# The scaled queries of the attention heads get the idle tiles of the raw weights' parts, and the first head's scores stand one unit later

## The chip, the cores and the metric

The kernel runs on one core of a Trainium2 chip. A core has a matrix engine (TensorE, PE in the profile, with PEld for its weight loads), three engines for elementwise work (VectorE is DVE, ScalarE is ACT, GpSimd is POOL) and a queue that issues the transfers from memory (SyncE, SP). Each engine carries out its own instructions in the order in which they were written for it, and waits on semaphores for the others. The metric is the time of one execution on the device in microseconds (us).

## The reference, cut to what matters

One layer of a streaming encoder works on 256 frames of width 2048 in float32: a half-step feed-forward part, a mixer, a cross attention over 256 memory tokens, and a second half-step feed-forward part. The change lies in the mixer:

```python
h = rms_norm(x, mix_norm[l])
proj = h @ w_in[l]
u, q, k, v, g, a_lr = jnp.split(proj, list(IN_SPLITS), axis=-1)
y_pool = pool_mixer(u, pool_w[l], pool_scale[l])
y_gla = gla_mixer(q, k, v, g, a_lr, gla_w_a2[l], gla_b_a[l], gla_head_norm[l])
x = x + jnp.concatenate([y_pool, y_gla], axis=-1) @ w_out[l]
```

The pool mixer takes, in four groups of channels, the trailing mean over 2, 4, 8 or 16 frames minus the frame itself, and multiplies each group with its own small matrix. The linear attention has four heads and works in four chunks of 64 frames: every frame of a chunk sees its whole chunk and all earlier ones, and each earlier chunk is weakened by the products of the decays in between.

## The kernel before, in words

**Units.** The whole kernel is one stream of units. A unit is one megabyte of weights: SyncE loads it into one of three `raw` tiles (`load`, line 1578), ScalarE rounds it to a high part `wh` (line 1602) and VectorE takes the difference to a low part `wl` (line 453), and TensorE multiplies with both parts, which gives a product near float32. The parts of two units ahead are made before the products of a unit are written (`AHEAD`, line 41), and there are three buffers of `wh` and `wl`, so the high part of a unit waits until TensorE is done with the unit three before it. Between the units stand operations that were handed in with `st.op(f, after)`: `f` is written `after` units later.

**Which instruction stands where on an engine.** The source is written in that order, but a planner then orders each engine's instructions by its own estimate of when they can start (line 1631). So an operation can be moved between the products of a unit. Parts of the weights keep their own order (`in_turn`).

**Tiles.** A pool tile has a tag and a number of buffers. A new tile with a tag takes the buffer whose last reader is done, and its first writer waits for that reader. In the mixer three buffers with the tag `m4` go round (`m4`, line 977). They hold the sums of the pool groups (`ev_pool`, line 986: the token tile `u` and two tiles `s0`, `s1` for the doubled sums), the intermediate results of the decay (`decay`, line 1067), the scaled queries of the heads (`scores`, line 1142) and the heads' outputs. In the profile all of these appear as `m`.

**Seven products.** Some units are multiplied with seven products in place of eight, and for these VectorE makes sums of the weights; the parts of the raw weights are then kept in tiles with the tags `xh` and `xl` (`split_seven`, line 471). In the mixer one tile of each stands ready (line 950), 128 x 1536 elements, and two units of the first block, which computes q and k, use them. After that block they have no use until the mixer ends.

**The order of the mixer.** q and k (block of eight units), the decay's low-rank gate, two blocks of four units for the pool groups (`block_a`, TensorE line 347, tile `pa`; each block ends with `ev_pool` of two groups), two blocks of four units for v (`block_b`, line 605, TensorE line 362, tile `pb`) with the pool's own weights as one unit in between (`pool_unit`, line 1018, TensorE line 1027, tile `pp`), and two blocks for the output gate. The scores of a head (`scores(h)`) copy and scale the queries into a tile with three copies on ScalarE (line 1150) and six multiplications on VectorE (line 1152), make four small float32 products on TensorE (line 1160, tile `pq`) and copy them out on VectorE (line 1166, tile `ST`).

**Where the change touches.** Before it, `scores(0)` is handed in with `after` 0. It stands between the last unit of the pool blocks and the first unit of v. The tile of its scaled queries is an `m4` tile.

## Time and profile before

| | us |
|---|---|
| median of three runs | 2090.24 |
| lowest, highest | 2089.54, 2092.51 |
| the profiled execution | 2089.89 |
| its span | 2088.1 |
| busy in the span: TensorE products | 2069.6 |
| busy in the span: VectorE | 1822.2 |
| busy in the span: ScalarE | 1152.4 |

The rows of the profile give times in us from the start of the span. A row of the timeline has a start, a length, engine, line, operation and tiles (result, arrow, operands), the number of instructions merged into it, and in brackets how long the engine stood idle before it and which instruction ended that. Names are those of the program without buffer numbers. PEclk is the share of the full clock that TensorE was granted.

### The profile page before, as it was taken

The numbers are of one execution on the slowest core, as the hardware profiler recorded it, in microseconds if no ns is written. First come the engines' busy times: TensorE is split into PE (matmuls) and PEld (weight loads), VectorE is DVE, ScalarE is ACT, GpSimd is POOL, SyncE is SP. The second block draws the span as 40 slices with busy tenths as digits, with TensorE's granted clock in tenths as the row PEclk, the third lists the DMA queues.
The fourth block names the chain that finished last, engine by engine and source line by source line (L and its number), as shares of the span: only waits on it lengthen the run. The fifth ranks groups of instructions, "written<-read, shape, count | busy, mean of one in ns | idle before, by whom it ended". The sixth has DMA issues, their size and how long they took to land.

```text
span 2088.1 us, 24282 instructions
## 1 busy us (share of the span) xinstructions
PE 2069.6 (99%) x9591; PEld 1724.6 (83%) x9591; DVE 1822.2 (87%) x1727; ACT 1152.4 (55%) x1151; POOL 100.1 (5%) x94
## 2 busy tenths in 40 slices
PE   9999999999999998999999999999999999999998
PEld 7888888888888887888888888888888888888886
DVE  7998899989998758579888887889988999889987
ACT  7655455645554664455756544566554556545554
POOL 0000000000000000000001000000100010000001
PEclk9999999999999999999999999999999999999999
DMA  7666666567666655557855555666576765676664
GB/s 263 204 200 225 237 222 220 183 222 243 222 200 223 230 176 161 162 173 231 270 193 172 172 184 178 205 204 229 188 233 205 242 208 196 225 236 227 206 227 152
DMA packets 129131, 435.94 MB, mean 209 GB/s; under 512 B 9845, under 2 KB 13529, under 8 KB 128633
## 3 DMA queue, kind: packets, MB, share of 16 engines
q1 hardware_dynamic: 128840, 433.86, 62.5%
q8 instruction: 75, 1.23, 0.2%
q10 hardware_dynamic: 176, 0.53, 0.1%
q14 instruction: 40, 0.32, 0.0%
HBM read 417.58 MB, written 16.78 MB: 208 GB/s over the span
## 4 chain that ended last, share of the span: by engine, by line
PE 98%; DVE 1%; DMA 0%; ACT 0%; issue 0%; SPq 0%; DVEq 0%; ACTq 0%
PE pt L362 59%; PE pt L507 28%; PE pa L347 4%; PE pb L362 2%; PE ph L780 1%; PE pl L1338 1%; PE pv L1375 1%; PE px L791 1%; DMA x<-in_x 0%; PE pp L1027 0%; PE pe L362 0%; DVE wl L453 0%; PE pq L1160 0%; PE pa L1054 0%; PE po L1173 0%; PE tm L1285 0%
## 5 line engine op out<-in xcount | busy, mean ns | idle before, releaser
L362 PE MATMUL pt<-wh,xs 128*128 128x512 f32 x2176 | 699.3, 391 | 0.0
L453 DVE TENSOR_TENSOR wl<-raw,wh 128x2048 fp32r<-128x2048 f32 (+1 forms) x249 | 534.0, 2152 | 117.0 <-ACT wh L1602 116.7
L1602 ACT CAST wh<-raw 128x2048 fp32r<-128x2048 f32 x249 | 475.4, 1912 | 263.3 <-PE pt L362 113.4
L362 PEld LDWEIGHTS pt<-wh,xs 128*128 128x128 f32 x2176 | 408.2, 188 | 83.7 <-ACT wh L1602 0.2
L489 ACT CAST wh<-T 128x1024 fp32r<-128x1024 f32 x250 | 262.5, 1054 | 376.1 <-DVE T L486 366.7
L362 PE MATMUL pt<-wh,ys 128*128 128x512 f32 x1440 | 455.1, 390 | 0.0
L362 PE MATMUL pt<-wl,xs 128*128 128x512 f32 x1088 | 424.8, 391 | 0.0
L362 PEld LDWEIGHTS pt<-wh,ys 128*128 128x128 f32 x1440 | 270.3, 188 | 55.6
L453 DVE TENSOR_TENSOR wl<-T,wh 128x2048 fp32r<-128x2048 f32 (+1 forms) x125 | 280.7, 2246 | 2.5 <-ACT wh L489 2.2
L362 PE MATMUL pt<-wl,ys 128*128 128x512 f32 x720 | 281.1, 391 | 0.0
L362 PEld LDWEIGHTS pt<-wl,xs 128*128 128x128 f32 x1088 | 204.6, 188 | 41.5
L280 DVE TENSOR_TENSOR xl<-raw,xh 128x1536 fp32r<-128x1536 f32 x125 | 218.9, 1751 | 13.6 <-ACT xh L279 13.5
L279 ACT CAST xh<-raw 128x1536 fp32r<-128x1536 f32 x125 | 185.0, 1480 | 59.1 <-PE pt L507 36.6
L486 DVE TENSOR_TENSOR T<-T,raw 128x512 f32<-128x512 f32 x250 | 172.5, 690 | 6.5
L362 PEld LDWEIGHTS pt<-wl,ys 128*128 128x128 f32 x720 | 135.2, 188 | 28.2 <-DVE wl L453 0.3
L486 DVE TENSOR_TENSOR T<-raw 128x1024 f32<-128x1024 f32 x125 | 152.3, 1218 | 0.5
L507 PE MATMUL pt<-wh,xs 128*128 128x512 f32 x380 | 147.9, 390 | 0.0
L457 POOL TENSOR_TENSOR wl<-raw,wh 128x768 fp32r<-128x768 f32 x42 | 78.0, 1857 | 1453.7 <-DVE wl L453 1444.6
L507 PE MATMUL pt<-xh,xs 128*128 128x512 f32 x384 | 143.4, 390 | 0.0
L507 PE MATMUL pt<-wh,xe 128*128 128x512 f32 x320 | 124.5, 389 | 0.0
L347 PE MATMUL pa<-xs,wh 128*128 128x512 f32 x256 | 90.7, 399 | 0.0
L507 PEld LDWEIGHTS pt<-xh,xs 128*128 128x128 f32 x384 | 72.1, 188 | 14.9
(256 smaller groups left out, 2360.0 us busy)
## 6 DMA issues: line engine op xcount, KB each, us to landing
raw<-in_ffn_w_down SPq DMA_DIRECT2D x88, 1024.0 KB, 5.5
raw<-in_ffn_w_up SPq DMA_DIRECT2D x80, 1024.0 KB, 5.0
raw<-in_ffn_w_gate SPq DMA_DIRECT2D x77, 1024.0 KB, 5.1
raw<-in_w_in SPq DMA_DIRECT2D x32, 1024.0 KB, 5.2
raw<-in_xattn_w_kv SPq DMA_DIRECT2D x32, 1024.0 KB, 5.1
raw<-in_w_out SPq DMA_DIRECT2D x16, 1024.0 KB, 5.6
raw<-in_xattn_w_q SPq DMA_DIRECT2D x16, 1024.0 KB, 5.5
raw<-in_xattn_w_o SPq DMA_DIRECT2D x16, 1024.0 KB, 5.5
```

What stands on the lines that cost most here:

```text
L279: in_turn("scalar", lambda: nc.scalar.copy(hi, src))
L280: in_turn("vector", lambda: nc.vector.tensor_tensor(out=lo, in0=src, in1=f32(hi), op=ALU.subtract))
L347: nc.tensor.matmul(o, w, x, start=k == 0 and i == 0, stop=last and i == 1)
L362: nc.tensor.matmul(ps, a, w, start=first and i == 0, stop=last and i == 2)
L453: in_turn("vector", lambda: nc.vector.tensor_tensor(out=lo[:, :n], in0=src[:, :n], in1=f32(hi[:, :n]), op=ALU.subtract))
L457: rest = nc.gpsimd.tensor_tensor(out=lo[:, n:], in0=src[:, n:], in1=f32(hi[:, n:]), op=ALU.subtract)
L486: in_turn("vector", lambda: nc.vector.tensor_tensor(out=o, in0=a, in1=b, op=ALU.add))
L489: in_turn("scalar", lambda: nc.scalar.copy(th[:, c], t[:, c]))
L507: nc.tensor.matmul(banks[n], x, w, start=n in fresh and j == 0, stop=n in ends and j == 2)
L780: nc.tensor.transpose(v[:, i, h * P : (h + 1) * P], g[:, h, i * P : (i + 1) * P], ident)
L791: nc.tensor.transpose(v[:, j, h * P : (h + 1) * P], x[:, h, j * P : (j + 1) * P], ident)
L1602: in_turn("scalar", lambda: nc.scalar.copy(hi, raw))
```

## The change

```diff
     def scores(h):
         q, kd, E, F = mix["q"][:, h, :], mix["k"][:, h, :], mix["E"], mix["F"]
 ...
-        QD = m4()
+        QD = scope["pool"].tile([P, 3 * NB], F32, tag=("xh", "xl")[h % 2], name=uid("QD"), bufs=1)
         at = (0, 3 * CH, 5 * CH)
 ...
-    for h, after in enumerate((0, 2, 4, 6)):
+    for h, after in enumerate((1, 2, 4, 6)):
         st.op(lambda h=h: scores(h), after)
```

The scaled queries of heads 0 and 2 go into the tile `xh`, those of heads 1 and 3 into `xl`. The `m4` buffers go round among the pool groups, the decay and the heads' outputs alone. The scores of head 0 are handed in one unit later, after the first unit of v.

No instruction is added or removed; their order changes. In the order written for the changed kernel:

- ScalarE has the copies of heads 0 and 1 right after the query tile itself, ahead of the decay's functions, those of head 2 behind the high part of v's fourth unit, and those of head 3 behind the high part of the pool's weights.
- VectorE has the twelve multiplications of heads 0 and 1 behind the factors of the decay, around the low part of the third unit of the second pool block and ahead of the low part of its fourth. The first multiplication of head 2 waits for the products of head 0, that of head 3 for those of head 1, since they take the same tile. The steps of the fourth pool group stand further apart: its first doubled sum behind the low part of v's fourth unit; the three others behind the copies (line 1166) of head 1, the multiplications of head 3 and the low part of the pool's weights; the means (lines 1001 and 1005) behind the low part of the next unit; and the group's own low part (line 286) behind the copies of head 2 and the low part of one more unit.
- TensorE goes from the last pool unit straight to the 24 products of v's first unit, then the undivided products of head 0, then v's second unit, the undivided products of head 1, v's third and fourth units, head 2, and the pool's unit. Of that unit, the products of the fourth group are split by products of the next unit of v: ten of them stand ahead of the first of the group, thirteen more ahead of the first that reads the group's low parts.
- SyncE and GpSimd have the same transfers and the same four clearings as before, in the same order.

## The prediction

> **What bounds the kernel now.** I read first the busy times and the shares of the chain that ended last:

> ```profile
> PE 2069.6 (99%) x9591; PEld 1724.6 (83%) x9591; DVE 1822.2 (87%) x1727; ACT 1152.4 (55%) x1151; POOL 100.1 (5%) x94
> PE 98%; DVE 1%; DMA 0%; ACT 0%; issue 0%; SPq 0%; DVEq 0%; ACTq 0%
> ```

> TensorE is the bound: 2069.6 us of products in a span of 2088.1, and 98% of the chain. A change gains only where TensorE stands still or runs slowly. So the next view is its waits, all of them:

> ```profile
> PE pq L1160 <- DVE m L1152: 6.6, 1, 6.6
> PE pwarm L206 <- POOL ident masks.py:199: 1.4, 1, 1.4
> PE px L717 <- DMA x<-in_x: 1.0, 1, 1.0
> PE pt L507 <- DVE xl L280: 0.2, 1, 0.2
> ```

> The columns are total, count and longest. One wait stands out: the first head's scores wait 6.6 us for their scaled queries. The timeline around it shows how it comes about:

> ```profile
> 804.52 0.39 PE L347 MATMUL pa<-xs,wh 128*128 128x512 f32 x1
> 804.88 0.69 DVE L319 TENSOR_TENSOR m<-pa,c 128x512 f32<-128x512 f32 x1
> 804.99 1.90 ACT L1602 CAST wh<-raw 128x2048 fp32r<-128x2048 f32 x1
> 806.40 0.72 DVE L997 TENSOR_TENSOR m<-m 128x542 f32<-128x542 f32 x1
> 807.04 2.29 DVE L453 TENSOR_TENSOR wl<-raw,wh 128x2048 fp32r<-128x2048 f32 x1
> 809.24 1.46 DVE L997 TENSOR_TENSOR m<-m 128x538 f32<-128x538 f32 x2
> 810.73 0.17 DVE L1001 SCALAR_TENSOR_TENSOR m<-m,invc 128x14 f32<-128x14 f32 x1
> 810.79 0.54 ACT L1150 COPY m<-q 128x64 f32<-128x64 f32 x3 [3.42 <-DVE m L997]
> 810.99 0.41 DVE L1152 TENSOR_SCALAR m<-q,F 128x64 f32<-128x64 f32 x2
> 811.54 1.08 PE L1160 MATMUL pq<-m,k 128*64 128x256 f32 x2 [6.63 <-DVE m L1152]
> ```

> The last pool product ends at 804.91. Only then can VectorE take it up (804.88 on), and the doubled sums of the third group hold the `m4` buffer that the queries need until 810.70. ScalarE's copies start at 810.79, the scores at 811.54. The products of v, which need nothing of this, stand behind the scores in TensorE's order. The table of stretches shows a second loss:

> ```profile
> 800.00:804.90 4.90, 4.90 (x28) 3.99 (x27) 3.01 (x3) 3.02 (x3) 0.00 (x0) 1.00 0.70 214
> 804.90:809.30 4.40, 0.01 (x1) 0.00 (x0) 4.26 (x5) 2.38 (x2) 0.00 (x0) 1.00 0.73 231
> 811.50:816.20 4.70, 4.66 (x11) 3.17 (x12) 3.51 (x8) 0.62 (x1) 0.12 (x1) 0.50 0.49 188
> 816.20:820.00 3.80, 3.80 (x21) 2.88 (x20) 0.83 (x2) 0.00 (x0) 0.00 (x0) 1.00 0.00 0
> ```

> The columns are the stretch, its length, busy times of PE, PEld, DVE, ACT and POOL, the granted clock, the DMA share and GB/s. From 811.50 to 816.20 the clock was 0.50: 11 products, where the next 3.8 us have 21.

> **The change part by part.** First, head 0's queries go into a tile that the pool does not use, and the scores stand one unit later. Both together take the wait of 6.63 us away, if v's first unit can start at 804.91. Its parts must be ready:

> ```profile
> 793.58 1.91 ACT L1602 CAST wh<-raw 128x2048 fp32r<-128x2048 f32 x1 [0.75 <-PE pa L347]
> 796.88 2.28 DVE L453 TENSOR_TENSOR wl<-raw,wh 128x2048 fp32r<-128x2048 f32 x1
> 802.46 2.29 DVE L453 TENSOR_TENSOR wl<-raw,wh 128x2048 fp32r<-128x2048 f32 x1 [1.12 <-ACT wh L1602]
> ```

> These are v's first unit (high part from 793.58, low part done at 799.16) and the low part of its second (done at 804.75); the third's is done at 809.33. So two units are ready when the pool block ends, 5.7 us of spare for the first, and the third is ready before it is due. The gain is the whole 6.63 us.

> Second, with no standstill there is no reason in the trace for the half clock: it lies nowhere else in this part. At 0.50, 4.66 us of work are worth 2.33. The gain is 2.3 us. [...]

> Third, the scores of heads 0 and 1 are no longer divided. The chain in order of time prices this:

> ```profile
> 812.63 5.99 PE pb L362 x18
> 819.21 8.61 PE pb L362 x37
> 827.82 0.57 PE pq L1160 x2
> 831.34 0.59 PE pq L1160 x5
> 838.72 0.80 PE pq L1160 x6
> 839.52 5.95 PE pp L1027 x48
> 845.47 5.47 PE pb L362 x24
> ```

> Head 1, in two pieces, takes 0.57 + 0.59 = 1.16; head 2, in one, takes 0.80. That is 0.36 for each of two heads, 0.7 in all. The first three rows check the clock: at 8.61 / 37 = 0.233 each, 18 products are 4.19, and with 1.16 for head 0 that is 5.35, while the chain has 819.21 − 811.54 = 7.67: 2.32 more.

> Fourth, the twelve multiplications of heads 0 and 1 move ahead of 804, where VectorE is busy. By the row of two in 0.41 us, one alone being 0.25, each adds 0.16: 1.9 us for twelve. What they delay is the low part of the last pool unit. It stands at

> ```profile
> 792.68 2.29 DVE L453 TENSOR_TENSOR wl<-raw,wh 128x2048 fp32r<-128x2048 f32 x1
> 800.65 0.69 DVE L286 TENSOR_TENSOR ys<-m,ys 128x512 fp32r<-128x512 f32 x1 [0.69 <-ACT ys L285]
> ```

> and ends at 794.97, with the multiplications at 796.9. The unit is due one unit before 804.91, about 5.6 us earlier by 24 products at 0.233, so at 799.3: 2.4 us of spare. Behind it VectorE has 0.69 and 1.12 us of idle time (800.65 and 802.46), which take up the delay. If the cover were gone it would cost 1.9 us. I take nothing. ScalarE's six copies move to a place where it waits for TensorE, and cost nothing: at 810.79 three take 0.54.

> Fifth, the new waits on VectorE. The first multiplication of head 2 waits for head 0's products. TensorE reaches their end at 804.91 + 5.59 + 0.80 = 811.3; VectorE stands there at 810.7, after the sums of the third group. It waits 0.6 us. Behind it are queued the copies of head 0, the fourth pool group and the low part of v's fourth unit. I add these up from the rows above and the following:

> ```profile
> 811.91 0.24 DVE L1152 TENSOR_SCALAR m<-q,E 128x64 f32<-128x64 f32 x1
> 819.17 0.72 DVE L997 TENSOR_TENSOR m<-m 128x538 f32<-128x538 f32 x1 [4.06 <-PE pq L1160]
> 819.81 1.32 DVE L1166 COPY ST<-pq 64x256 f32<-64x256 f32 x4
> 838.76 1.27 ACT L1137 ACTIVATE v<-pb,Rcol 128x512 f32<-128x512 f32 x2 [3.53 <-PE pb L362]
> 812.03 0.62 ACT L285 CAST ys<-m 128x512 fp32r<-128x512 f32 x1 [0.70 <-DVE m L1005]
> ```

> From 811.3: six multiplications 1.05, line 1001 0.17, three half-tile steps 2.07 (0.69 each), copies of head 0 1.32, low part 2.29. It ends at 818.2. The unit is due after units two and three and head 1: 811.3 + 5.59 + 0.80 + 5.59 = 823.3. Spare: 5 us.

> The tightest chain is the fourth pool group, whose low part now stands late. VectorE goes on from 818.2: low part of the third group and first sum 1.41, copies of head 1 1.32, head 3 1.05, the pool's weights 2.29, three sums 2.16, a low part 2.29, means 0.86, so 829.6. Head 2's products end on TensorE at 823.3 + 5.59 + 0.80 = 829.7; its copies 1.32 more, 831.0. The next low part waits for ScalarE, which first takes v out of TensorE's result (from 828.9, 1.27) and then rounds (1.90), to 832.1; then 2.29 and 0.69: 835.1. ScalarE writes the group's high part at 832.1 + 0.62 = 832.7. TensorE begins the pool's unit at 829.7. At 5.95 / 48 = 0.124, 36 products bring it to 834.2, ten products of v to 836.5, where it needs the high part (3.8 us of spare); a first product or two and thirteen more of v to 839.7, where it needs the low part (4.6 us of spare). If the cover were gone, it would cost what is missing.

> The products of v amid those of the pool make some more changes of tile on TensorE. Between the last two rows of the chain above (839.52 + 5.95 = 845.47) such a change costs nothing; from 0.80 − 0.57 the most I would give is 0.1 for each of four. I take 0.1 in all.

> SyncE and GpSimd keep their orders. In the standstill the transfers ran at 231 GB/s and after it at 0; without it, a unit of one megabyte is used in about 5.6 us, which is 187 GB/s, below the 214 GB/s of the stretch before. A raw tile is reloaded when its low part is made, and I have those spare times above.

> Sum: −6.6 − 2.3 − 0.7 + 0.1 = −9.5 us. The profiled execution took 2089.89, so 2080.4; the median, 2090.24, stands 0.35 above it, and would give 2080.7. I say **2080.5 us**.

> **The rivals.** *The half clock stays.* If it came from something else here, such as the small products, the gain would be 6.6 + 0.7 − 0.1 = 7.2: 2083.0. Against it: heads 2 and 3 have the same small products and the clock stays at full in

> ```profile
> 820.00:840.00 20.00, 20.00 (x96) 15.51 (x95) 15.31 (x35) 9.08 (x16) 0.00 (x0) 1.00 0.39 116
> ```

> *A shorter wait in its place.* VectorE carries out what stands behind a waiting instruction only after it, as the 4.06 us at 819.17 show, where a pool sum waited for head 0's products. Now two first multiplications wait for TensorE. If the steps behind take some 5 us longer than I added, TensorE waits for a low part. A wait of 1 to 4 us leaves 2081.5 to 2084.5; I put it at 2083. [...]

> *No gain.* If v's first unit were not ready, or its result had no free bank, TensorE would wait there as long: 2090. Against it are the low part at 799.16, and that VectorE has read the pool results of the block before, whose bank it takes, long ago:

> ```profile
> 785.39 0.68 DVE L319 TENSOR_TENSOR m<-pa,c 128x512 f32<-128x512 f32 x1
> ```

> *Slower.* The low part of the fourth pool group is so late that TensorE stands still longer than now. With the clock's 2.3 us, the wait must be over 9.5 + 4.2 − 2.3 = 11.4 us to end 4.2 us above now, so the low part must come 16 us later than 835.1. At 12 us it would be 2095. Nothing in these rows is that late.

> **How the numbers follow.** 0.2% is 4.2 us, about what a measurement of this kernel can tell from no change. The forecast, 2080.5 (2079 to 2082 alone), has a chance of 0.80; the half clock that stays 0.06; the shorter wait 0.08; no gain 0.03; slower 0.03. Faster is 0.80 + 0.06 + 0.08 = 0.94, same 0.03, slower 0.03. The range reaches down by 2 us for prices too low (the crossing, a longer slow stretch) and up over the half clock's and the shorter wait's 2083: 2078.5 to 2083.5.

> **What would show it.** TensorE's waits have no line 1160, and the granted clock is 1.00 from 800 to 830. The products of v begin at about 805.1. The first row of the chain for head 0 is about 0.80, undivided. The span is about 2078.5. VectorE has a wait of about 0.6 us for TensorE at line 1152 near 811. I am wrong if TensorE waits at line 1027 for line 286 or 285, or at line 362 for a low part between 805 and 850, or if the slow clock stays.

## The result, and the profile after

| | before, us | changed, us |
|---|---|---|
| median of six runs each | 2090.22 | 2079.27 |
| lowest, highest | 2088.17, 2092.51 | 2078.92, 2080.34 |
| profiled execution, and its span | 2089.89, 2088.1 | 2080.34, 2078.6 |

The changed kernel is faster: its time is 0.9948 of the time before, 95% interval 0.9935 to 0.9961. By the medians that is 10.95 us. 2080.5 was predicted, with a range of 2078.5 to 2083.5.

Busy times and the shares of the chain, from the page of the changed kernel:

```profile
PE 2065.9 (99%) x9591; PEld 1722.5 (83%) x9591; DVE 1821.8 (88%) x1727; ACT 1152.6 (55%) x1151; POOL 100.0 (5%) x94
PE 99%; DMA 0%; DVE 0%; ACT 0%; SPq 0%; issue 0%; DVEq 0%; ACTq 0%
```

The same 9591 products; VectorE and ScalarE do the same work. TensorE is busy 3.7 us less, 3.3 of it in the part shown below, where none of its products runs on the slow clock any more and heads 0 and 1 are in one piece; its share of the chain rises from 98% to 99%. All the waits of TensorE (total, count, longest):

```profile
PE px L717 <- DMA x<-in_x: 1.8, 1, 1.8
PE pwarm L206 <- POOL ident masks.py:199: 1.4, 1, 1.4
PE pt L507 <- DVE xl L280: 0.2, 1, 0.2
```

The wait at line 1160 is gone and none has come in its place. The first row, at the start of the kernel, was 1.0 before and is 1.8 here: in this execution the input came later, and the pool blocks end at 805.38 in place of 804.91. Three stretches around the old standstill, again with the granted clock behind the five busy times:

```profile
804.90:809.30 4.40, 4.40 (x21) 3.65 (x20) 4.26 (x5) 2.80 (x3) 0.00 (x0) 1.00 0.74 230
809.30:811.50 2.20, 2.20 (x15) 1.54 (x13) 1.82 (x3) 0.58 (x1) 0.12 (x1) 1.00 0.29 55
811.50:816.20 4.70, 4.70 (x22) 3.87 (x21) 4.46 (x15) 2.38 (x5) 0.00 (x0) 1.00 0.55 207
```

The clock is 1.00 in all, and the stretch that had 11 products has 22. The chain in order of time through this part (start, length, what):

```profile
795.85 9.53 PE pa L347 x54
805.37 5.46 PE pb L362 x24
810.84 0.79 PE pq L1160 x6
811.63 5.67 PE pb L362 x24
817.30 0.80 PE pq L1160 x6
818.10 11.11 PE pb L362 x48
829.21 0.80 PE pq L1160 x6
830.00 4.51 PE pp L1027 x36
834.52 2.29 PE pb L362 x10
836.81 0.23 PE pp L1027 x2
837.04 2.97 PE pb L362 x13
840.02 1.19 PE pp L1027 x10
841.21 0.23 PE pb L362
841.44 0.79 PE pq L1160 x6
842.23 5.66 PE pb L362 x24
```

It is TensorE alone, one piece ending where the next begins, each head in one piece of 0.79 or 0.80. Before, the last of these rows began at

```profile
851.73 5.67 PE pb L362 x24
```

From the end of the pool blocks that is 851.73 − 804.91 = 46.8 us before and 842.23 − 805.38 = 36.9 us now: 10.0 us less for the same work. The wait made 6.6 of it and shorter times of the products the other 3.3.

### The profile page after: what moved, and what is told of

It reads as the page before. It is cut to its first block, busy times and chain, and to the rows that moved or that the text cites. A ratio compares the mean times of both kernels' runs of the same rounds, so it can differ in the third digit from the quotient of the medians.

```text
span 2078.6 us, 24269 instructions
## 1 busy us (share of the span) xinstructions
PE 2065.9 (99%) x9591; PEld 1722.5 (83%) x9591; DVE 1821.8 (88%) x1727; ACT 1152.6 (55%) x1151; POOL 100.0 (5%) x94
## 4 chain that ended last, share of the span: by engine, by line
PE 99%; DMA 0%; DVE 0%; ACT 0%; SPq 0%; issue 0%; DVEq 0%; ACTq 0%
PE pt L362 59%; PE pt L507 28%; PE pa L347 4%; PE pb L362 2%; PE ph L780 1%; PE pl L1338 1%; PE pv L1375 1%; PE px L791 1%; DMA x<-in_x 0%; PE pp L1027 0%; PE pe L362 0%; PE pa L1054 0%; PE po L1173 0%; PE tm L1285 0%; PE px L717 0%; PE pq L1160 0%
## 5 line engine op out<-in xcount | busy, mean ns | idle before, releaser
L362 PE MATMUL pt<-wh,xs 128*128 128x512 f32 x2176 | 698.5, 390 | 0.0
L453 DVE TENSOR_TENSOR wl<-raw,wh 128x2048 fp32r<-128x2048 f32 (+1 forms) x249 | 533.7, 2151 | 110.5 <-ACT wh L1602 110.3
L1602 ACT CAST wh<-raw 128x2048 fp32r<-128x2048 f32 x249 | 475.3, 1912 | 259.7 <-PE pt L362 113.5
L362 PEld LDWEIGHTS pt<-wh,xs 128*128 128x128 f32 x2176 | 407.9, 188 | 83.7 <-ACT wh L1602 0.2
L362 PE MATMUL pt<-wh,ys 128*128 128x512 f32 x1440 | 454.7, 389 | 0.0
L362 PE MATMUL pt<-wl,xs 128*128 128x512 f32 x1088 | 424.1, 390 | 0.0
L362 PEld LDWEIGHTS pt<-wh,ys 128*128 128x128 f32 x1440 | 270.2, 188 | 55.6
L453 DVE TENSOR_TENSOR wl<-T,wh 128x2048 fp32r<-128x2048 f32 (+1 forms) x125 | 280.6, 2245 | 2.5 <-ACT wh L489 2.2
L362 PE MATMUL pt<-wl,ys 128*128 128x512 f32 x720 | 280.7, 390 | 0.0
L362 PEld LDWEIGHTS pt<-wl,xs 128*128 128x128 f32 x1088 | 204.5, 188 | 41.6
L280 DVE TENSOR_TENSOR xl<-raw,xh 128x1536 fp32r<-128x1536 f32 x125 | 218.8, 1750 | 13.6 <-ACT xh L279 13.5
L362 PEld LDWEIGHTS pt<-wl,ys 128*128 128x128 f32 x720 | 135.2, 188 | 28.4 <-DVE wl L453 0.4
L507 PE MATMUL pt<-wh,xs 128*128 128x512 f32 x380 | 147.7, 389 | 0.0
L507 PE MATMUL pt<-xh,xs 128*128 128x512 f32 x384 | 143.2, 389 | 0.0
L507 PE MATMUL pt<-wh,xe 128*128 128x512 f32 x320 | 124.3, 389 | 0.0
L347 PE MATMUL pa<-xs,wh 128*128 128x512 f32 x256 | 90.7, 398 | 0.0
L507 PEld LDWEIGHTS pt<-xh,xs 128*128 128x128 f32 x384 | 72.1, 188 | 14.9
```

What stands on the lines that cost most here:

```text
L280: in_turn("vector", lambda: nc.vector.tensor_tensor(out=lo, in0=src, in1=f32(hi), op=ALU.subtract))
L347: nc.tensor.matmul(o, w, x, start=k == 0 and i == 0, stop=last and i == 1)
L362: nc.tensor.matmul(ps, a, w, start=first and i == 0, stop=last and i == 2)
L453: in_turn("vector", lambda: nc.vector.tensor_tensor(out=lo[:, :n], in0=src[:, :n], in1=f32(hi[:, :n]), op=ALU.subtract))
L507: nc.tensor.matmul(banks[n], x, w, start=n in fresh and j == 0, stop=n in ends and j == 2)
L1602: in_turn("scalar", lambda: nc.scalar.copy(hi, raw))
```

## The experiments

Two groups of four kernels ran, each group on one chip beside the kernel before: the first four below beside a median of 2089.09, the last four beside 2089.26. My theory is that of the prediction: a wait for a shared buffer, a half clock that follows from the standstill, and two heads in pieces.

**Only the tile.**

```diff
-    for h, after in enumerate((1, 2, 4, 6)):
+    for h, after in enumerate((0, 2, 4, 6)):
```

on the changed kernel.

> The scaled queries go into xh and xl as in the changed kernel, but the first head's scores stay ahead of v's first unit. My theory: the 6.6 us wait came from the shared m4 buffer alone, so the queries are ready long before 804.9, TensorE has no wait at line 1160, the granted clock stays at 1.00, and the time is that of the changed kernel within 1 us: 2079 to 2080.5. Rival: the move by one unit carries the gain (the scores also wait for something else at that place, such as the scaled keys or the free result bank); then TensorE still waits there for several us and the time is over 2085.

Measured: 2079.45, ratio 0.9953 (0.9939 to 0.9966), 9.6 us below before. Its chain:

```profile
794.96 9.87 PE pa L347 x56
804.83 0.79 PE pq L1160 x6
805.63 11.11 PE pb L362 x48
```

The scores follow the pool blocks with nothing in between: TensorE has no wait at line 1160, and the granted clock is 1.00 from 800 to 840. The other tile alone gives the gain; the move by one unit is not needed for it.

**Only the move.**

```diff
-    for h, after in enumerate((0, 2, 4, 6)):
+    for h, after in enumerate((1, 2, 4, 6)):
```

on the kernel before.

> The queries stay in m4 buffers, the first head's scores stand one unit later. In the written order the fourth pool group now takes the m4 buffers first, and the scores of heads 0 and 1 come behind all four units of v. My theory, that only v's products have to be free to start: the wait of 6.6 us and the half clock are gone here too, the time is some 8 us below before, 2081 to 2083, with one or two waits of about 1 us for the queries between v's last unit and the pool's unit, below what halves the clock. Rival, that the buffer is what matters: the wait only moves, TensorE waits 4 us or more for the queries at the later place, the clock falls to half there and the time is 2087 to 2092.

Measured: 2081.54, ratio 0.9965 (0.9952 to 0.9977), 7.6 us below before and 2.1 above the tile alone. The row of its waits, and pieces of its chain:

```profile
PE pq L1160 <- ACT m L1150: 1.8, 1, 1.8
```

```profile
803.88 21.80 PE pb L362 x96
...
826.29 0.68 ACT v L1137
826.97 1.79 ACT wh L1602
828.76 0.15 ACT m L1150
...
828.96 0.65 PE pq L1160 x2
...
831.83 0.58 PE pq L1160 x5
```

All four units of v run at once, so the long wait and the half clock are gone (the granted clock is 1.00 from 800 to 840). In their place head 2 waits 1.8 us for ScalarE's copies, which stand in ScalarE's order behind v's results and a high part, and it is divided: 0.65 + 0.58 in place of 0.79. These are 1.8 + 0.4 = 2.2, about the 2.1 between the two medians. So the move alone also frees v, but only the tile keeps the later heads' queries out of the way.

**The standstill filled: 48 transposes.**

```diff
+    st.op(lambda: spare_transposes(48))
     for h, after in enumerate((0, 2, 4, 6)):
```

on the kernel before. Their result is not used.

> The kernel before with 48 unused transposes on TensorE ahead of the first scores, about 5.2 us of work at 0.108 us each, in the place where it stood still. The wait for the queries stays, cut to some 1.4 us. My theory: the half clock came from the standstill and is gone, which is worth 2.3 us: 2087.9, between 2087 and 2089, with a granted clock of 1.00 from 800 to 830. Rival: the half clock comes from something else at that place; then it stays at 0.50 for some 5 us behind the wait, and the time is 2090 to 2091.

Measured: 2086.39, ratio 0.9986 (0.9977 to 0.9995), 2.7 us below before, though the queries come no earlier. One row of its waits and three of its chain:

```profile
PE pq L1160 <- DVE m L1152: 1.4, 1, 1.4
```

```profile
810.80 0.62 PE pq L1160 x2
816.40 0.58 PE pq L1160 x5
827.64 0.80 PE pq L1160 x6
848.24 5.67 PE pb L362 x24
```

The clock is 1.00 in every stretch from 800 to 840, so the half clock came from the standstill. By the medians alone the gain is loosely known (the interval reaches from 1.0 to 4.8 us), but the chain shows it as well: from the start of head 0's products to the end of head 3's it takes 851.73 − 811.54 = 40.2 us before and 848.24 − 810.80 = 37.4 here, 2.75 less. Not all of this is the clock's. The planner also put head 1 in one piece here, 0.80 in place of 1.16. And a piece of v's products that follows a head's products is 0.2 us longer than one that does not: in the changed kernel 24 products take 5.67 there, and 5.46 behind the pool block. I call these 0.2 us a restart; why they arise the rows do not show. An undivided head saves one, so head 1 is worth 0.36 + 0.2 = 0.56, and 2.2 of the 2.75 us are the clock's.

**The standstill filled less: 12 and 24 transposes.** The same edit with 12.

> The same with 12 transposes, about 1.3 us, so TensorE still stands still for some 5.3 us. My theory: 5.3 us are enough to halve the clock, as 6.6 us were (it fell 4.4 us after the standstill began), so the half clock stays for 4 to 5 us and the time is that of before, 2090 within 1 us. Rival: any work in the gap keeps the clock; then it is 2088 as with 48 transposes.

Measured: 2089.34, ratio 1.0001 (0.9992 to 1.0010): no difference, as my theory had it, though the half clock lasted 5.9 us behind the wait and not the 4 to 5 that I gave. With 24:

> The kernel before with 24 unused transposes ahead of the first scores, about 2.6 us, so TensorE stands still for some 4.0 us. The clock fell 4.5 us after the standstill began in the kernel before and 4.4 us after it with 12 transposes. If it takes that long, 4.0 us are not enough, the clock stays at 1.00 and the time is that of 48 transposes, 2.7 us below before. [...]

Measured: 2088.46, ratio 0.9996 (0.9987 to 1.0005), by the medians 0.8 us below before, between the cases of 12 and of 48. The waits and stretches of the two, 12 first:

```profile
PE pq L1160 <- DVE m L1152: 5.3, 1, 5.3
809.30:811.50 2.20, 0.58 (x2) 0.29 (x2) 2.13 (x9) 0.63 (x4) 0.01 (x1) 0.66 0.63 167
811.50:816.20 4.70, 4.70 (x12) 3.40 (x11) 2.89 (x7) 0.53 (x1) 0.12 (x1) 0.50 0.37 145
816.20:820.00 3.80, 3.80 (x19) 2.76 (x19) 0.85 (x2) 0.00 (x0) 0.00 (x0) 0.92 0.00 0
```

```profile
PE pq L1160 <- DVE m L1152: 4.0, 1, 4.0
809.30:811.50 2.20, 0.64 (x2) 0.28 (x2) 2.17 (x8) 0.69 (x4) 0.07 (x1) 0.86 0.64 166
811.50:816.20 4.70, 4.70 (x16) 3.50 (x15) 2.82 (x6) 0.46 (x1) 0.05 (x1) 0.70 0.38 146
```

If the clock is either full or half, a granted clock of c over a stretch means that a share 2(1 − c) of it ran at half. The kernel before bears the condition out: of its twenty stretches of half a microsecond from 808 to 818, eighteen show 1.00 or 0.50, and only the two in which the clock changes show 0.88 and 0.79. With 12: 1.5 + 4.7 + 0.6 = 6.8 us. With 24: 0.6 + 2.8 = 3.4 us, the half. My reading, that 4.0 us of standstill are too short, fell. In the profiled execution the clock did fall, at the end of the standstill, and stayed low for 3.4 us, half as long as with 12.

**The changed kernel again**, beside the next two.

> The changed kernel itself, beside the others of this group on one chip. No wait at line 1160, clock at 1.00 from 800 to 860, and a time 9.5 to 10 us below before: by the chain of its first profile the first three heads take 0.79 to 0.80 us each, and from the end of the pool blocks to the end of head 3 it is 10.0 us shorter than before.

Measured: 2079.07, ratio 0.9952 (0.9940 to 0.9965), 10.2 us below before.

**More waiting on VectorE: one tile for all heads.**

```diff
-        QD = scope["pool"].tile([P, 3 * NB], F32, tag=("xh", "xl")[h % 2], name=uid("QD"), bufs=1)
+        QD = scope["pool"].tile([P, 3 * NB], F32, tag="xh", name=uid("QD"), bufs=1)
```

> The changed kernel with the queries of all four heads in the one tile xh, so each head's first multiplication on VectorE waits for the products of the head before. In the written order head 1's products come eight products of v later. My theory, that VectorE's waits of this kind lie in spare time of some 4 us: no wait on TensorE, the time of the changed kernel within 1 us. Rival, the shorter wait that takes the place of the one removed: what is queued on VectorE behind the wait comes late, TensorE waits 1 to 4 us for a low part or for the queries, and the time is 1 to 4 us above the changed kernel.

Measured: 2079.50, ratio 0.9954 (0.9941 to 0.9968). VectorE's idle time ahead of line 1152 is now

```profile
  PE pq L1160: 1.5, 2
```

against one wait of 0.5 in the changed kernel. TensorE has no wait in this part, and head 1 stands eight products later (810.65 + 7.49 = 818.14) in one piece:

```profile
810.65 7.49 PE pb L362 x32
818.14 0.79 PE pq L1160 x6
```

Three times the waiting on VectorE costs nothing that can be measured: it lies in spare time.

**The fourth pool group made late.**

```diff
+            if g == 3:
+                for _ in range(16):
+                    nc.vector.tensor_copy(src[:, :, PAD:], src[:, :, PAD:])
             split_pair(ys, 8 + 2 * g, src[:, :, PAD:])
```

on the changed kernel.

> The changed kernel with sixteen unused copies of the fourth pool group's means onto themselves on VectorE, ahead of its parts: at most 16 x 0.69 = 11 us later. In the written order the products of this group then stand behind the attention of head 0, some 14 us later. My theory: the planner moves v's products ahead, so the cover is larger than the 4.6 us that I gave, and the time stays within 1 us of the changed kernel. Rival, the slower case: TensorE waits for the group's low part, over 4.4 us with the half clock behind it, 5 us or more above the changed kernel.

Measured: 2079.26, ratio 0.9954 (0.9940 to 0.9967). The group's low part on VectorE and its products on TensorE (line numbers of this kernel are three higher from here on, so 1030 is line 1027):

```profile
844.35 0.69 DVE L286 TENSOR_TENSOR ys<-m,ys 128x512 fp32r<-128x512 f32 x1 [0.69 <-ACT ys L285]
```

```profile
848.05 0.24 PE pp L1030 x2
...
848.52 1.19 PE pp L1030 x10
```

The low part ends at 845.0. Counted from the end of the pool blocks, which is 803.85 here, it comes 11 us later than in the changed kernel, though the sixteen copies are shorter than I had expected: about 0.43 us each, 7.0 in all. The planner had put the products of v, of head 0's output and of half of head 1's ahead of the group's, which begin at 848.05, and TensorE does not wait. It knew of the delay when it wrote the order, so this shows how far the cover can be stretched, not what an unforeseen delay would cost.

## Why the prediction was right

- *The wait of 6.63 us.* Right, and its cause with it: the tile alone removes it. Of the two halves of the change I had called both together the reason; the first would have done.
- *The half clock, 2.3 us.* Right: it goes with the standstill, and the chain with 48 transposes prices it at 2.75 − 0.56 = 2.2. The rival that it stays is out.
- *The divided heads, 0.7 us.* Right in kind, but too small. Heads 0 and 1 take 0.79 and 0.80, against 1.16. The prediction priced only these pieces; each division also makes one restart of v's products more, 0.2 us, so the term is 2 x 0.56 = 1.1.
- *VectorE's order.* Its wait for head 0's products was to be 0.6 us. The rows of the changed kernel's timeline, all about 0.5 us late with this execution:

```profile
793.05 2.28 DVE L453 TENSOR_TENSOR wl<-raw,wh 128x2048 fp32r<-128x2048 f32 x1
798.00 2.29 DVE L453 TENSOR_TENSOR wl<-raw,wh 128x2048 fp32r<-128x2048 f32 x1
811.67 0.25 DVE L1152 TENSOR_SCALAR QD<-q,E 128x64 f32<-128x64 f32 x1 [0.51 <-PE pq L1160]
815.89 2.29 DVE L453 TENSOR_TENSOR wl<-raw,wh 128x2048 fp32r<-128x2048 f32 x1
832.20 0.62 ACT L285 CAST ys<-m 128x512 fp32r<-128x512 f32 x1
834.54 0.68 DVE L286 TENSOR_TENSOR ys<-m,ys 128x512 fp32r<-128x512 f32 x1
```

  The wait was 0.51. v's fourth low part was to end at 818.2 and ended at 818.2, which is 0.5 earlier than given by this execution's clock; the fourth group's high part at 832.7 and came at 832.8, its low part at 835.1 and came at 835.2. TensorE first read them at 836.8 and 840.0, where 836.5 and 839.7 were given: 4.0 and 4.8 us of spare, where 3.8 and 4.6 were given. The delay of up to 1.9 us for the last pool unit's low part did not come: it ended at 795.33, by this execution's clock 0.1 us earlier than before, because steps of the first two pool groups moved behind it.
- *The changes of tile on TensorE, +0.1 us.* They cost next to nothing: the pool's unit and v's unit in six pieces take 841.44 − 830.00 = 11.44 us, and in two pieces before 5.95 + 5.47 = 11.42.
- *The sum, −9.5 us.* The part measures −10.0. The term that was mis-sized is that of the divided heads, 1.1 in place of 0.7. The prediction's check of the clock hid this: it took a product of v at 0.233 us, from 37 products in 8.61, and that piece holds a restart. In the changed kernel 24 take 5.46 where there is none, 0.2275 each. With that, 18 products are 4.10, head 0 in two pieces 1.16 and the restart between them 0.2, which together is 5.46 as well; the chain had 7.67, so the slow clock cost 2.21 in place of 2.3. So 6.63 + 2.21 + 1.12 = 9.96, and the part measures 9.97. The two errors, +0.4 and −0.1, are small beside the intervals of the medians. The profiled execution shows 9.5 in its span only because it started 0.5 us late; that it came out at 2078.6, where about 2078.5 was given, is luck to that extent. That the median fell by 10.95 in the first comparison and by 10.2 in the second is within their intervals.

## What to carry to other kernels

On an engine that does its work in the order written, as TensorE does here, one instruction that waits for a buffer holds up all work behind it, however ready that is: v's first unit, its low part done at 799.16, stood behind the wait of 6.63 us that ended at 811.54. Look for the ready work, and then either give the waiting step another buffer, one that is free in time, or put it behind the ready work. Here each of the two took most of the 10 us, and only the buffer took all. Price a standstill of TensorE by its length and by the clock behind it: filling it with useless products already brought back 2.7 us, some 2.2 of them the clock's.

## What was not expected of the hardware

```profile
809.30:811.50 2.20, 0.00 (x0) 0.00 (x0) 2.13 (x8) 0.54 (x3) 0.00 (x0) 0.52 0.42 89
```

which is 2.1 us, with 4.7 behind it. So its length does not follow the length of the standstill in a simple way: in the profiled executions one of 4.0 in place of 5.3 halves it. Counted back from 811.5 by the share of this stretch that ran at half, the clock fell at 809.4 in the kernel before (2.1 us of it), at 810.0 with 12 transposes (1.5) and at 810.9 with 24 (0.6). TensorE resumed at 811.54, 810.92 and 810.86. So the clock fell 2.2 and 0.9 us before TensorE resumed in the two cases of 6.8 us, and just as TensorE resumed in the case of 3.4. With one execution of each profiled, what sets the length is not settled. Nor need the 3.4 us hold for every execution with 24 transposes: of the ten, five list a mean clock over the span of 0.998 (2087.55 to 2088.61 us, the profiled one among them) and five 0.997 (2088.38 to 2089.56), and 3.4 us more at half would lower that mean by 0.0008.
